# First weights side by side in one array, first products by kind, and sums of squares through transposes, in a one-core encoder layer

## The chip, the core and the metric

The kernel runs on one core of one Trainium2 chip. A core has five engines, each with an instruction queue of its own: TensorE (PE in the profile; PEld is its loading of weights) multiplies matrices into PSUM, VectorE (DVE) and ScalarE (ACT) do element-wise work, GpSimd (POOL) does element-wise work more slowly, SyncE (SP) only issues transfers. Transfers between the chip's memory (HBM) and the core's memory (SBUF) are made by 16 DMA engines; SP and ACT put them on their queues. The metric is the device time of one execution in microseconds (us), as a median of several runs; lower is better.

## The reference

One layer of an encoder on 1024 tokens of width 1024, in float32:

```python
hn   = rmsnorm(h, norm_mix)
proj = hn @ w_in                       # 18 tiles of 128 columns
o_a  = window_gqa_sink(...)            # |i-j| <= 128, a sink logit for each head
o_b  = neighbourhood_attention(...)    # 8 x 16 window on a 16 x 64 grid
mix  = concat(rmsnorm(o_a, norm_a), rmsnorm(o_b, norm_b))
h    = h + mix @ w_out
hn   = rmsnorm(h, norm_ffn)
h    = h + (silu(conv3(hn @ w_gate)) * (hn @ w_up)) @ w_down
out  = rmsnorm(h, norm_final)
```

`rmsnorm(x, g)` is `x / sqrt(mean(x*x) + 1e-6) * g` over the 1024 (or 512) features of a token. `proj` is split into the parts of both attention groups; group A rotates part of each head. All other details are the same in both kernels and play no part here.

## The kernel before

**Layout and products.** Features lie on the 128 partitions and tokens along the rows: `xT` is eight tiles `xts[k]` of 128 x 1024. A float32 product is made as three products of a rounded type: each operand is split into a high part (ACT rounds it) and a low part (DVE subtracts), and `block` (lines 167 to 170) adds high weight by high x, high weight by low x, and low weight by high x into one PSUM bank, each for 512 tokens. `tsl(h)` is half h of the tokens. So one weight tile needs, for each k and half, three matrix products with 512 columns.

**The start.** The first three tiles of `w_in` (projections 0, 1 and 2, the list `first`) are not run one after another but side by side, k by k, as x arrives, into six PSUM banks (two each with the tags `pj`, `o`, `s`). Lines 84 to 122 write the transfers: `w_in` is laid out as [tile, partition, k, column], so each of the three tiles has its own transfers, for k=0, k=1, k=2..3 and k=4..7 (`steps`), between the transfers of x. All are issued by SP, but the second half of `xts[0]` and `par` (120 columns of small parameters: norm gains, convolution weights) by ACT. `pin` keeps the marked instructions in the written order on their queues. Lines 580 to 621 write the splits: `split_x` scales x by the gain from `par` and splits it, `split_first_w` splits the weights of one tile and step (ACT the high part, DVE the low part), and `add_square` squares each x tile on ACT and adds up the squares on DVE in `acc`. Nine warm-up products (`WARM`, line 137) run on PE before the first operands are there.

The products are written in lines 636 to 649: for k=0 to 5 both halves and three tiles, then the last two k (`TAIL`) tile by tile. After the first tile's first half come two calls of `inverse_narrow` on `acc`; after the second tile's first half come two of `widen`.

**The norms.** `inverse_narrow` (lines 194 to 204) turns a tile of squares (features on partitions, tokens along the row) into `1/sqrt(mean + eps)` with tokens on partitions: for each block of 128 tokens a matrix product with the squares as the stationary operand and one column of `ones` (each 1/1024), a square root on ACT and a reciprocal on DVE. `widen` spreads that back over all partitions with a transpose for each block. The calls are: a pair for the first norm, a pair for group A (`narrow_a`, `wide_a`), a pair for group B (lines 841 to 847), a single one for each half of the second norm (lines 953 and 1099), one for a half of the last norm (line 1368), and two with n=2 and two tiles of squares each for the quarters of the other half (lines 1385 and 1390).

**The end.** The last product of `w_down` for the second four output tiles is made in two quarters of 256 tokens. `leave_quarter` adds a quarter of PSUM to the residual and squares it into `parts`; for the tile before the last it also adds the sum of the squares of all earlier tiles. `finish` widens the norm twice (DVE reads one bank, ACT copies the other for GpSimd), scales and issues the output.

**What sets the order.** PE's instructions run exactly in the order in which they are written (line 127). Instructions of ACT, DVE, POOL and SP that aren't pinned are put in order ahead of time by a planner, from estimated times and priorities; `tc.high_priority(offset)` moves an instruction ahead in it, `tc.issue_after` behind a named one. In the attention stage, projections fill in between attention units by rates written out by hand (`RATES`). The SBUF pools have a fixed number of buffers for each tag: 8 `mix` and 14 `op` tiles of 128 x 1024, 2 `raw`, 3 `whi`, 3 `wlo`.

## Time and profile before

| | |
|---|---|
| median of 3 runs | 1087.69 us (1087.55 to 1088.12) |
| the profiled execution | 1088.62 us, its span 1086.8 us |
| instructions | 14983, of them 5144 matrix products |
| mean granted clock of PE | 0.997 |
| busy share of the span | PE 98%, weight load 82%, DVE 79%, ACT 51%, POOL 10% |
| DMA | 144.94 MB moved, mean 133 GB/s |

The span runs from the first to the last instruction of the profiled execution; all row times below count from its start. A row of the timeline reads: start in us, duration in us, engine, line of the kernel, operation, what it writes `<-` what it reads, shape, and how many neighbouring instructions of that kind the row merges; in brackets the idle time of the engine in front of it and what ended it. SPq and ACTq are the issuing of transfers. Durations of matrix products overlap, since they are pipelined; the distance from start to start is what one costs. The lines themselves stand in the prediction.

### The profile page before, as it was taken

To read this page: it belongs to the slowest core of one execution; us is meant where nothing else is said; L and a number is where in the kernel's file an instruction comes from. 1 tells how busy PE (TensorE), PEld (TensorE's weight loads), DVE (VectorE), ACT (ScalarE), POOL (GpSimd) and SP (SyncE) were. 2 spreads that over 40 slices of the span, in tenths; PEclk is the share of its full clock that TensorE was granted. 3 is DMA by queue.
4 is the path that set the end of the run, shared out by engine and by line. 5 is a ranking of instruction groups with operands and counts; after the bars stand their busy time and mean duration, and the time that the engine had idled before them with its cause. 6 is when DMAs were issued, how large, how long until landed. Compare 5 with 4: busy or idle time off the path is not lost.

```text
span 1086.8 us, 14983 instructions
## 1 busy us (share of the span) xinstructions
PE 1070.2 (98%) x5144; PEld 895.0 (82%) x5144; DVE 860.1 (79%) x1570; ACT 554.5 (51%) x1047; POOL 105.0 (10%) x188
## 2 busy tenths in 40 slices
PE   8999999999999999999999999999999999999997
PEld 7888888888888888887788888888888888888887
DVE  6789787667788688899998877877887867897764
ACT  7457676556676545545434334342433645444451
POOL 0223332222232100000000000000000000000001
PEclk9999999999999999999999999999999999999998
DMA  8223022232225147214342222323322788867644
GB/s 275 73 73 88 30 68 59 78 77 78 78 68 161 65 137 249 88 39 157 134 146 107 107 107 97 120 95 111 111 88 97 244 297 295 272 214 241 227 129 155
DMA packets 69084, 144.94 MB, mean 133 GB/s; under 512 B 8208, under 2 KB 19600, under 8 KB 69008
## 3 DMA queue, kind: packets, MB, share of 16 engines
q1 hardware_dynamic: 58784, 118.43, 34.6%
q10 hardware_dynamic: 10224, 25.56, 6.2%
q8 instruction: 40, 0.66, 0.3%
q14 instruction: 36, 0.29, 0.1%
HBM read 103.58 MB, written 28.57 MB: 122 GB/s over the span
## 4 chain that ended last, share of the span: by engine, by line
PE 88%; DVE 8%; ACT 2%; DMA 1%; issue 1%; SPq 0%; POOL 0%; DVEq 0%; ACTq 0%; POOLq 0%
PE pj L168 7%; PE pj L169 7%; PE pj L170 7%; PE dn L883 6%; PE dn L885 6%; PE dn L884 6%; PE z L885 5%; PE z L884 5%; PE z L883 5%; PE s L344 3%; PE x L883 3%; PE x L884 3%; PE x L885 3%; PE y L885 3%; PE y L884 3%; PE y L883 3%
## 5 line engine op out<-in xcount | busy, mean ns | idle before, releaser
L872 ACT ACTIVATE whi<-ws 128x512 fp32r<-128x512 f32 (+1 forms) x100 | 60.3, 623 | 127.8 <-DVE ws L990 80.5
L883 PE MATMUL dn<-xd,whi 128*128 128x512 f32 (+1 forms) x330 | 124.1, 376 | 0.0
L885 PE MATMUL dn<-xd,wlo 128*128 128x512 f32 (+1 forms) x330 | 123.7, 375 | 0.0
L884 PE MATMUL dn<-xd,whi 128*128 128x512 f32 (+1 forms) x330 | 123.7, 375 | 0.0
L168 PE MATMUL pj<-xgh,whi 128*128 128x512 f32 x248 | 104.4, 421 | 1.0 <-ACT xgh L584 1.0
L885 PE MATMUL z<-hg,wlo 128*128 128x512 f32 x264 | 103.0, 390 | 0.7 <-DVE wlo L873 0.7
L883 PE MATMUL z<-hg,whi 128*128 128x512 f32 x264 | 102.9, 390 | 0.0
L884 PE MATMUL z<-hg,whi 128*128 128x512 f32 x264 | 102.7, 389 | 0.0
L370 ACT ACTIVATE p<-p,nm 128x385 f32<-128x385 f32 (+3 forms) x128 | 75.1, 587 | 50.4 <-DVE nm L366 49.3
L169 PE MATMUL pj<-xgl,whi 128*128 128x512 f32 x248 | 97.5, 393 | 0.9 <-DVE xgl L585 0.8
L170 PE MATMUL pj<-xgh,wlo 128*128 128x512 f32 x248 | 97.6, 394 | 0.0
L374 POOL TENSOR_SCALAR p<-p,sm 128x384 f32<-128x384 f32 (+1 forms) x128 | 74.9, 598 | 219.3 <-DVE sm L372 204.7
L873 DVE TENSOR_TENSOR wlo<-raw,whi 128x512 fp32r<-128x512 f32 (+1 forms) x102 | 66.4, 671 | 26.6 <-ACT whi L872 26.4
L872 ACT ACTIVATE whi<-raw 128x512 fp32r<-128x512 f32 (+1 forms) x102 | 60.6, 612 | 45.2 <-DMA raw<-in_w_down_dram 20.0
L873 DVE TENSOR_TENSOR wlo<-ws,whi 128x512 fp32r<-128x512 f32 (+1 forms) x100 | 66.9, 681 | 21.0 <-ACT whi L872 20.8
L380 DVE TENSOR_TENSOR pl<-pt,ph 128x384 fp32r<-128x384 f32 (+2 forms) x108 | 63.3, 589 | 24.3 <-ACT ph L379 23.0
L1307 POOL TENSOR_TENSOR h<-h,wide 128x256 f32<-128x256 f32 (+1 forms) x6 | 5.4, 924 | 709.9 <-ACT wide L1303 709.9
L379 ACT ACTIVATE ph<-pt 128x384 fp32r<-128x384 f32 (+2 forms) x108 | 55.2, 514 | 32.2 <-PE pt L479 25.1
L885 PEld LDWEIGHTS dn<-xd,wlo 128*128 128x128 f32 x330 | 62.1, 188 | 11.3
L884 PEld LDWEIGHTS dn<-xd,whi 128*128 128x128 f32 x330 | 62.1, 188 | 11.1
L883 PEld LDWEIGHTS dn<-xd,whi 128*128 128x128 f32 x330 | 62.1, 188 | 11.1
L1198 ACT ACTIVATE xd<-xd 128x512 fp32r<-128x512 f32 x77 | 47.5, 626 | 44.0 <-DMA xd<-x 43.2
(220 smaller groups left out, 2671.2 us busy)
## 6 DMA issues: line engine op xcount, KB each, us to landing
xd<-x SPq DMA_DIRECT2D x77, 256.0 KB, 4.6
raw<-in_w_down_dram SPq DMA_DIRECT2D x72, 256.0 KB, 3.6
raw<-in_w_gate_dram SPq DMA_DIRECT2D x22, 512.0 KB, 3.4
raw<-in_w_up_dram SPq DMA_DIRECT2D x22, 512.0 KB, 3.8
x<-c ACTq DMA_DIRECT2D x22, 512.0 KB, 3.5
raw<-in_w_in_dram SPq DMA_DIRECT2D x30, 256.0 KB, 2.9
raw<-in_w_down_dram SPq DMA_DIRECT2D x36, 192.0 KB, 3.8
x<-t ACTq DMA_DIRECT2D x11, 512.0 KB, 2.6
```

Source lines behind the costliest of these rows:

```text
L168: nc.tensor.matmul(ps, w[0], x[0][:, tsl(h)], start=first, stop=False)
L169: nc.tensor.matmul(ps, w[0], x[1][:, tsl(h)], start=False, stop=False)
L170: nc.tensor.matmul(ps, w[1], x[0][:, tsl(h)], start=False, stop=last)
L370: nc.scalar.activation(p[:, j, 0:e], p[:, j, 0:e], AF.Exp, bias=nm, scale=-1.0, accum_out=sm[:, j:j + 1])
L374: nc.gpsimd.tensor_scalar(p[:, i, 0:m], p[:, i, 0:m], sm[:, i:i + 1], 1.0, op0=ALU.mult, op1=ALU.mult)
L379: nc.scalar.activation(ph[:, 0:n], ps[:, 0:n], AF.Copy)
L380: nc.vector.tensor_tensor(pl[:, 0:n], ps[:, 0:n], f32(ph[:, 0:n]), op=ALU.subtract)
L872: nc.scalar.activation(hi, src, AF.Copy)
L873: nc.vector.tensor_tensor(lo, src, f32(hi[:, :, :]), op=ALU.subtract)
L883: nc.tensor.matmul(ps, w[0], x[0], start=first and i == 0, stop=False, skip_group_check=True)
L884: nc.tensor.matmul(ps, w[0], x[1], start=False, stop=False, skip_group_check=True)
L885: nc.tensor.matmul(ps, w[1], x[0], start=False, stop=last and i == len(ws) - 1, skip_group_check=True)
```

## The change

The change has six parts.

1. The weights of the first three tiles leave `w_in` for an array of their own, `w_first`, laid out as [partition, k, 384]: for each k the 128 columns of all three tiles lie side by side. Five transfers (k=0, 1, 2..3, 4..5, 6..7) replace twelve. The raw tiles and the splits move to other buffers (two `raw`, three `op`, five `mix`). `w_in` starts at tile 3.
2. Of `par`, the eight columns of the first norm's gain are loaded first, by ACT's queue; the other 112 after them, also there. The second half of `xts[0]` goes to SP's queue. The order of loads is x0 first half, w0, x0 second half, w1, x1 in halves, w2..3, x2, x3, w4..5, x4, x5, w6..7, x6, x7.
3. The first weights are split for each k in one piece of 384 columns, k=0 with the high part on DVE, just ahead of that k's x.
4. The first half of k=0 is multiplied by kind: high by high for three tiles, then low weight by high x, then high weight by low x. Warm-up products fall from nine to seven.
5. `inverse_narrow` with a single tile of squares transposes the blocks on PE, sums them on DVE along the row, and takes root and reciprocal as before, all with high priority; with two tiles it stays as it was. The copy of the first norm (`rstd1`) also gets high priority.
6. At the end, `finish` widens once unless it is the last quarter's. For the first quarter `leave_quarter` adds the last tile's squares to those of the tile before, so that the quarter's norm has a single tile of squares; it is made after the second of three groups in place of the first, and `finish` after the third in place of the second.

```diff
-WARM = 9
+WARM = 7
...
-        steps = [slice(0, 1), slice(1, 2), slice(2, 4), slice(4, 8)]
-        load_x(0, tsl(0))
-        nc.scalar.dma_start(par[:, 0:C_SINK], small)
-        load_x(0, tsl(1), nc.scalar)
-        for m in range(3):
-            load_first_w(m, steps[0])
...
+        FIRST = [slice(0, 1), slice(1, 2), slice(2, 4), slice(4, 6), slice(6, 8)]
...
+        def load_first_w(i):
+            ks = FIRST[i]
+            pin(nc.sync.dma_start(raws[i], w_first[:, ks, :]))
+
+        pin(nc.scalar.dma_start(par[:, 0:KT], small[:, 0:KT]))
         load_x(0, tsl(0))
+        load_first_w(0)
+        load_x(0, tsl(1))
+        load_first_w(1)
         load_x(1, tsl(0))
         load_x(1, tsl(1))
+        load_first_w(2)
+        for i, k in ((3, 2), (4, 4)):
             load_x(k)
+            load_x(k + 1)
+            load_first_w(i)
+        load_x(6)
+        load_x(7)
+        pin(nc.scalar.dma_start(par[:, KT:C_SINK], small[:, KT:C_SINK]))
...
         def inverse_narrow(sqs, dim, tag, n=4):
             ps = bank("ss", tag)
+            v = cpool.tile([128, n], F32, name="v4", tag="v4", bufs=4, padded_shape=[128, 4])
+            if len(sqs) == 1:
+                for c in range(n):
+                    nc.tensor.transpose(ps[:, c * 128:(c + 1) * 128], sqs[0][:, c * 128:(c + 1) * 128], ident)
+                with tc.high_priority(offset=500):
+                    nc.vector.tensor_reduce(v, ps[:, 0:n * 128].rearrange("p (c w) -> p c w", w=128), axis=mybir.AxisListType.X, op=ALU.add)
+                    nc.scalar.activation(v, v, AF.Sqrt, bias=eps, scale=1.0 / dim)
+            else:
+                for i, sq in enumerate(sqs):
+                    for c in range(n):
+                        nc.tensor.matmul(ps[:, c:c + 1], sq[:, c * 128:(c + 1) * 128], ones[:, 0:1], start=c == 0 and i == 0,
+                                         stop=i == len(sqs) - 1, skip_group_check=True)
+                with tc.high_priority(offset=500):
+                    nc.scalar.activation(v[:, 0:n], ps[:, 0:n], AF.Sqrt, bias=eps, scale=float(D) / dim)
+            with tc.high_priority(offset=500):
+                nc.vector.reciprocal(v[:, 0:n], v[:, 0:n])
             return v
...
+        def hi_first_w(k, queue):
+            i, raw = next((i, r) for i, r in enumerate(FIRST) if r.start <= k < r.stop)
+            raw = raws[i][:, k - raw.start]
+            if queue is nc.vector:
+                pin(queue.tensor_copy(his[k], raw))
+            else:
+                pin(queue.activation(his[k], raw, AF.Copy))
+            return raw
+
+        def split_first_w(k, queue=nc.scalar):
+            raw = hi_first_w(k, queue)
+            pin(nc.vector.tensor_tensor(los[k], raw, f32(his[k]), op=ALU.subtract))
...
+        split_first_w(0, nc.vector)
         split_x(0, tsl(0))
         split_x(0, tsl(1))
+        split_first_w(1)
         for h in range(2):
             split_x(1, tsl(h))
         acc = add_square(xts[0], None)
         for k in range(2, KT):
+            split_first_w(k)
             split_x(k)
             acc = add_square(xts[k - 1], acc)
...
+        for part in range(3):
+            for p, ps in zip(first, banks):
+                w, x = p.w[0], xg[0]
+                nc.tensor.matmul(ps[0], w[part == 1], x[part == 2][:, tsl(0)], start=part == 0, stop=False)
         for k in range(KT - TAIL):
-            for h in range(2):
+            for h in range(k == 0, 2):
...
-            wide, again = widen(v, "pt", n), widen(v, "pt", n)
+            wide = widen(v, "pt", n)
+            again = widen(v, "pt", n) if split else wide
...
             if j + NP < KT - 1:
                 nc.vector.tensor_tensor(s2, s2, sq[0][:, cols], op=ALU.add)
+            elif cols.start == 0:
+                nc.vector.tensor_tensor(s2, s2, parts[0, j - 1], op=ALU.add)
...
-                    if (k, j, c) == (1, 2, 0):
-                        vs[0] = inverse_narrow([parts[0, 2], parts[0, 3]], D, "s", 2)
                     if (k, j, c) == (1, 2, 1):
+                        vs[0] = inverse_narrow([parts[0, 3]], D, "s", 2)
+                    if (k, j, c) == (1, 2, 2):
                         finish(0, vs[0], quarters[0])
...
+        "w_first": w_in[0:3].transpose(1, 2, 0, 3).reshape(128, KT, 384),
+        "w_in": w_in[3:],
```

More of the change, by code (lines that the diff above doesn't have):

```diff
@@ L89, in load_x @@
             pin(queue.dma_start(xts[k][:, part], xT[k, :, part]))
-        def halves(name, dt=F32):
-            t = big(name, "mix", dt)[:, :].rearrange("p (k c) -> p k c", c=128)
-            return t[:, 0:4], t[:, 4:8]
-        raws = [wpool.tile([128, 4, 128], F32, name="raw", tag="raw", bufs=2) for _ in range(2)]
-        his, los = ([wpool.tile([128, 4, 128], F32R, name=n, tag=n) for _ in range(3)] for n in ("whi", "wlo"))
-        (r3, r3b), r12, h12, l12, (h3, l3) = halves("r3"), halves("r12"), halves("h12", F32R), halves("l12", F32R), halves("w3", F32R)
@@ L111, in hybrid_layer @@
-        for m in range(3):
-            load_first_w(m, steps[1])
+        FIRST = [slice(0, 1), slice(1, 2), slice(2, 4), slice(4, 6), slice(6, 8)]
+        flat = lambda t, n: t[:, 0:n * 384].rearrange("p (k c) -> p k c", c=384)
+        raws = [wpool.tile([128, HALF], F32, name="raw", tag="raw", bufs=2) for _ in range(2)]
+        raws = [flat(t[:, :], 1) for t in raws] + [flat(big("r", "op")[:, :], 2) for _ in range(3)]
+        his, los = ([wpool.tile([128, HALF], F32R, name=n, tag=n)[:, 0:384] for _ in range(3)] for n in ("whi", "wlo"))
```

50 lines of the change are left out of this document (15 added, 35 removed).

## The prediction

> **What bounds the kernel now.** I read the page's engine shares and chain, then who TensorE (PE) waited for, then the start row by row, since the change lies there and at nine short reductions.
>
> ```profile
> PE 1070.2 (98%) x5144; PEld 895.0 (82%) x5144; DVE 860.1 (79%) x1570; ACT 554.5 (51%) x1047; POOL 105.0 (10%) x188
> PE 88%; DVE 8%; ACT 2%; DMA 1%; issue 1%; SPq 0%; POOL 0%; DVEq 0%; ACTq 0%; POOLq 0%
> ```
>
> PE is busy for 98% of the 1086.8 us span and makes 88% of the chain that ended last. Its order is written by hand, so a PE instruction that goes away moves all behind it forward, as long as nothing else comes late. The waits of PE:
>
> ```profile
> PE o L491 <- DVE pl L380: 1.4, 4, 0.6
> ...
> PE pj L168 <- ACT xgh L584: 1.0, 1, 1.0
> PE pj L169 <- DVE xgl L585: 0.8, 1, 0.8
> ```
>
> The columns are total us, times and the longest. The first is the largest of the attention stage, the last two are the start, which in order of time reads:
>
> ```profile
> 0.74 0.39 SPq L89 DMA_DIRECT2D xt<-in_xT_dram  x1
> ...
> 4.00 0.72 ACT L584 ACTIVATE xgh<-xt,par 128x512 fp32r<-128x512 f32 x1 [0.84 <-DMA par<-in_small_dram]
> ...
> 4.97 0.50 PE L168 MATMUL pj<-xgh,whi 128*128 128x512 f32 x1
> ...
> 6.14 0.39 PE L168 MATMUL o<-xgh,whi 128*128 128x512 f32 x1
> ...
> 6.74 0.90 SPq L89 DMA_DIRECT2D xt<-in_xT_dram  x2
> ...
> 13.44 0.39 PE L170 MATMUL s<-xgh,wlo 128*128 128x512 f32 x1
> 13.58 1.15 ACT L584 ACTIVATE xgh<-xt,par 128x1024 fp32r<-128x1024 f32 x1 [1.61 <-DMA xt<-in_xT_dram]
> ...
> 14.76 1.28 DVE L585 SCALAR_TENSOR_TENSOR xgl<-xt,par,xgh 128x1024 fp32r<-128x1024 f32 x1 [3.29 <-ACT xgh L584]
> ...
> 16.10 0.50 PE L169 MATMUL pj<-xgl,whi 128*128 128x512 f32 x1 [0.82 <-DVE xgl L585]
> ...
> 32.45 1.21 DVE L597 TENSOR_TENSOR sq<-sq 128x1024 f32<-128x1024 f32 x1
> ...
> 33.71 1.95 PE L199 MATMUL ss<-ones,sq 128*128 128x1 f32 x16
> ...
> 35.52 0.47 PE L168 MATMUL pj<-xgh,h 128*128 128x512 f32 x1
> ...
> 35.99 0.18 DVE L203 RECIPROCAL v<-v 128x4 f32<-128x4 f32 x1 [0.72 <-ACT v L202]
> ```
>
> The third tile of x (k=2) lands at 13.58, and PE stands until its high and low parts are made. From the first product at 4.97 to the first reduction at 33.71 PE needs 28.74 us for 114 products (six k of 18, and six of the last two k). From 6.14 to 13.44 there are 32 steps without a gap, 0.228 us each; at that pace 26.0 would do, and 2.7 are lost. VectorE (DVE) meanwhile makes the low parts and the running sum of squares, which that reduction reads; its last addition ends at 33.66.
>
> ```profile
> 3.00:11.00 8.00, 7.91 (x36) 6.53 (x35) 4.80 (x12) 5.33 (x15) 0.00 (x0) 1.00 0.95 269
> 11.00:14.00 3.00, 2.82 (x13) 2.01 (x11) 0.43 (x1) 1.39 (x3) 0.00 (x0) 1.00 0.99 360
> 14.70:33.70 19.00, 18.11 (x78) 14.56 (x78) 18.94 (x19) 15.88 (x19) 3.59 (x2) 1.00 0.57 210
> ```
>
> In these windows the columns are length, busy us of PE, weight load, DVE, ACT and POOL, granted clock, DMA share and GB/s. Before 14.7 the transfers are the limit (DMA share 0.95 and 0.99); after it DVE is, busy for 18.94 of 19.00. So the start has two limits, and gaining on PE alone stops at DVE.
>
> **Part 1, the loads.** Twelve weight loads become five, x's second half goes from ACT's queue to SP's, and SP issues 15 transfers instead of 21. Two small loads, 8 columns and then 112, take the place of one on ACT's queue. Ahead of k=2 SP had 12 issues from 0.74 to 6.74, 0.5 each; now it has seven, so k=2 is issued at about 4.2, 2.5 earlier. If issuing decided alone, k=2 would land near 11.0. By bytes, x0, x1, x2 and the weights of four k come first, with the small parameters: 2.42 MB, before and after. The sum of the GB/s rows reaches that at about 11 us, and k=2 was seen 2.5 later. Without the hole that the issues leave, the 360 GB/s of the second window bounds the rate from above and 269 from below. With 0.25 MB moved by 3.0, the bytes are there between 9.0 and 11.0; with 1.5 to 2.5 for the landing this gives 10.5 to 13.5. I take 11.5, between the issue bound and the bytes, a gain of 2.1.
>
> **Part 2, the splits.** DVE's chain to the first reduction moves with k=2, but its weights grow: per k one low part of 128x384 where three tiles' halves stood.
>
> ```profile
> 10.21 0.75 DVE L590 TENSOR_TENSOR wlo<-raw,whi 128x256 fp32r<-128x256 f32 x2
> ...
> 18.29 1.29 DVE L590 TENSOR_TENSOR l<-r,h 128x512 fp32r<-128x512 f32 x2
> ```
>
> Two overlap a little, which gives 0.35 or so a piece for 256 columns and 0.6 for 512, so 0.48 for 384, an estimate. From k=2 on, five of them (k=3 to 7) are 2.4 where three 512s took 1.8: +0.6. The last addition ends at 33.66 - 2.1 + 0.6 = 32.16. PE's own path is shorter. The first operands come with less in front of them: `par` falls from 120 columns (60 KB) to 8 (4 KB), and the 0.84 of ACT's wait for it goes or shrinks, but ACT now needs x and DVE the first weights, so I let the first product start at 4.7 (4.4 to 5.2). Running all `hi` by `hi` products first, then `lo` weights, then `lo` x gives DVE 1.4 us before its slowest result is due, so the stalls at 5.2 to 6.1 go. PE reaches the reduction at 4.7 + 26.0 + 0.3 = 31.0 and waits for DVE until 32.16. Gain at that point 33.71 - 32.16 = **1.55**. Bounds: 2.7 if DVE isn't the limit, -0.45 if k=2 lands at 13.5 again. Two fewer warm-up products (WARM) cost nothing while operands are later than their end.
>
> **Part 3, the sums.** A single reduction of four column blocks was four products with a one-column operand, two records each. It becomes four transposes, a DVE sum and the same root and reciprocal.
>
> ```profile
> 277.56 1.84 PE L199 MATMUL ss<-ones,sq 128*128 128x1 f32 x16
> 279.27 0.48 PE L168 MATMUL pj<-xgh,whi 128*128 128x512 f32 x1
> ...
> 423.09 0.95 PE L199 MATMUL ss<-ones,s 128*128 128x1 f32 x8
> 423.90 0.49 PE L168 MATMUL pj<-mgh,wo 128*128 128x512 f32 x1
> ...
> 38.37 1.03 PE L210 MATMUL sw<-cst,v 128*128 128x128 f32 x8
> 39.16 0.47 PE L168 MATMUL o<-xgh,h 128*128 128x512 f32 x1
> ...
> 426.76 0.60 PE L210 MATMUL sw<-cst,v 128*128 128x128 f32 x4
> 427.12 0.48 PE L168 MATMUL pj<-mgh,wo 128*128 128x512 f32 x1
> ```
>
> From start to start, a pair of reductions takes 1.81 at 33.71 and 1.71 at 277.56, a single one 0.81; eight transposes take 0.79, four 0.36. There are three pairs (first norm, group A, group B): (1.81 - 0.79) + 2 x (1.71 - 0.79) = 2.86. Three singles (both halves of the second norm, one of the last): 3 x 0.45 = 1.35. Together **4.2** of PE. The Trainium skill, "TensorE: Matmul & The Clock Gate", Part 4, speaks against this edit: it gives about 275 ns for a transpose in a kernel. By that the 36 transposes would cost 9.9, more than the products that they replace, and the 4.2 would be a loss of about 2. This trace disagrees: 0.79 / 8 is 0.10 each, so I give that outcome no chance.
>
> Each single reduction adds one DVE sum out of PSUM, 128x512; the nearest rows are a subtraction and an addition from SBUF (L590 some 0.65 for 512, L597 1.21 for 1024), so 0.7. Its cover is the PE work between reduction and widening: 12 products, 2.7 us, at the first norm; the same 12 at group B, 2.9 us at 423.90 to 426.76, more elsewhere. At the first norm a pair's second reciprocal now ends 36.17 - 33.71 = 2.46 after the pair began; less 1.02 of products and with 0.7 for the sum that is 2.1 after the start and 1.35 after the transposes, 2.05 if the second sum has to follow the first. Either fits; each 0.1 that it is late costs 0.1. Behind the sums on DVE's queue stand evacuations and splits, which PE waits for at a few places only (above). Nothing to 3.5 in all, rival (d); I take 0.
>
> **Part 4, the end.** The first quarter's reduction of two sums becomes one of two transposes, after one more DVE addition, and is made one group later.
>
> ```profile
> 1059.55 1.03 PE L210 MATMUL sw<-cst,v 128*128 128x128 f32 x8
> 1060.35 0.36 PE L883 MATMUL dn<-xd,whi 128*128 128x256 f32 x1
> ...
> 1069.77 0.95 PE L199 MATMUL ss<-ones,s 128*128 128x1 f32 x8
> 1070.59 0.36 PE L883 MATMUL dn<-xd,whi 128*128 128x256 f32 x1
> ...
> 1072.52 2.44 DVE L1309 SCALAR_TENSOR_TENSOR h<-h,par,sw 128x256 f32<-128x256 f32 x6 [1.29 <-PE sw L210]
> ...
> 1080.42 2.44 DVE L1309 SCALAR_TENSOR_TENSOR h<-h,par,sw 128x256 f32<-128x256 f32 x6 [0.63 <-PE sw L210]
> ```
>
> The reduction falls from 0.82 to 0.18 (two transposes): 0.64. The second widening is dropped: 0.80 to 0.36 for the half, 0.36 to 0.18 for the quarter: 0.62. Against it, only nine 256-column products (1.1, half the pace's 0.228 each) now lie between reduction and widening, and the chain of 1.35, with a sum of half the width (-0.3), takes 1.05 to 1.25: -0.1. What hangs on that widening (DVE's scaling, GpSimd, eight output transfers on SP's queue) moves one group, 1.1, later; the last quarter's own scaling starts 7.9 after the first's, so they keep clear. The last quarter keeps its form. Sum **1.15**.
>
> **Sum.** 1.55 + 4.2 + 1.15 = 6.9. The profiled execution took 1088.62 (span 1086.8), 0.93 over the median of the runs, so 1081.7 as it was taken and **1080.8** as a median: 1087.69 - 6.9.
>
> **Rivals.** (a) *Transfers keep their pace*, k=2 lands near 13.5. For: DMA share 0.95 already. Against: the issues spread over six us. Term of the start -0.45: 1082.8.
> (b) *DVE isn't the limit of the start*, because fewer, longer instructions or a better place for other weights' splits save it a microsecond. Term 2.7: 1079.6.
> (c) *PE starts cold.* The warm-up's weight loads are slow:
>
> ```profile
> L138 PEld LDWEIGHTS warm_ps<-ones x18: 288/333/338, 1.0 to 4.6; 128*128 128x128 f32 x18
> L199 PEld LDWEIGHTS ss<-ones,sq x48: 186/192/192, 33.7 to 382.5; 128*128 128x128 f32 x48
> ```
>
> 333 ns against 192 for the same form later, and only the last is quicker, so the array speeds up at about 4.8, after 3.8 us of work, though the granted clock reads 1.00. Fourteen records instead of 18 end at 4.1. If the pause to 4.7 starts the count again, 3.8 us run at half pace: 1.9 lost, of which the 1.15 that PE waits for DVE anyway absorbs most: 1081.6. The Trainium skill, same page, Part 1, has this rule (half rate until one busy window of some 3.4 us); by its figure the loss would be 1.7 before absorption.
> (d) *The sums come late*: DVE serves them behind other work and PE waits 0.5 at each of seven widenings, 3.5: 1084.3. For: DVE 79% busy. Against: high priority, covers of 2.7.
> (e) *Slower: the attention stage loses its fit.* ACT, DVE and POOL instructions that aren't pinned are put in order by a planner from estimated times; new ones change that. PE's place to lose is the wait of the second value product (L491) for `pl`:
>
> ```profile
> L380 DVE TENSOR_TENSOR pl<-pt,ph 128x384 fp32r<-128x384 f32 (+2 forms) x108 | 63.3, 589 | 24.3 <-ACT ph L379 23.0
> ```
>
> It is made 108 times, and four waits for it average 0.35. It decides from 20 further waits of that size (7.0). At a third of the 108 it costs 12.6: 1093.4. Against: PE's order and the stage's balance stay, and the edit touches one pair of sums in it.
>
> **Numbers.** Forecast 0.50, (a) 0.14, (b) 0.12, (c) 0.06, (d) 0.10, (e) 0.08. The range 1078.8 to 1085.0 holds the first five with the bounds of the start and of the sums; (e) and a bad (d) lie outside. A measurement here tells 0.2% (2.2 us) from no change: faster 0.86, the same 0.06 (the part of (d) and a mild (e) above 1085.5), slower 0.08.
>
> **What would show it.** Right: k=2's first ACT row near 11.5; PE reaching the first reduction near 32, with a wait for the sum of squares; pairs of transposes of 0.79; no PE wait of over 0.3 at a widening but the last two. Wrong: k=2 near 13.5; new waits at L491 or at a widening; first products 0.43 apart.

## The result and the profile after

| | before | after |
|---|---|---|
| median | 1087.72 us (1086.77 to 1088.12, 6 runs) | 1082.76 us (1082.01 to 1083.54, 6 runs) |
| the profiled execution | 1088.62, span 1086.8 | 1082.01, span 1080.2 |
| ratio of the runs | | 0.9955, 95% interval 0.9944 to 0.9967 |

The kernel became 4.96 us faster, where 6.9 were forecast. The two profiled executions lie 6.6 apart: before's is 0.90 above its median, after's 0.75 below its own. By the two profiles' pages PE still makes most of the chain. Of the changed kernel:

```profile
PE 1064.6 (99%) x5092; PEld 889.0 (82%) x5092; DVE 866.3 (80%) x1578; ACT 553.8 (51%) x1042; POOL 103.6 (10%) x188
PE 85%; DVE 9%; ACT 3%; DMA 1%; issue 1%; POOL 0%; DVEq 0%; SPq 0%; ACTq 0%; POOLq 0%
```

PE lost 5.6 us of busy time (1070.2 to 1064.6) and 52 products; DVE and ACT have a larger share of the chain. Whom PE waited for (us in total, times, longest):

```profile
PE o L501 <- DVE pl L390: 1.5, 4, 0.6
PE vt L307 <- DVE pl L390: 1.4, 2, 1.1
...
PE sw L220 <- DVE v L213: 1.1, 3, 0.6
```

The waits for k=2 of x (1.0 and 0.8 before) are gone, the two of the attention stage stand as they were (1.5 and 1.4, before 1.4 and 1.4), and the widenings `sw` now wait three times, 1.1 in all, where they waited once, 0.6. The start in order of time:

```profile
5.22 0.63 PE L653 MATMUL o<-xgh,whi 128*128 128x512 f32 x1
...
5.65 0.63 PE L653 MATMUL s<-xgh,whi 128*128 128x512 f32 x1
...
6.36 0.39 PE L653 MATMUL o<-xgh,wlo 128*128 128x512 f32 x1
...
10.31 1.15 ACT L594 ACTIVATE xgh<-xt,par 128x1024 fp32r<-128x1024 f32 x1
11.50 1.28 DVE L595 SCALAR_TENSOR_TENSOR xgl<-xt,par,xgh 128x1024 fp32r<-128x1024 f32 x1 [0.73 <-ACT xgh L594]
...
29.71 1.21 DVE L617 TENSOR_TENSOR sq<-sq 128x1024 f32<-128x1024 f32 x1
...
31.32 1.03 PE L201 MATMUL ss<-cst,sq 128*128 128x128 f32 x8
...
32.11 0.48 PE L169 MATMUL pj<-xgh,h 128*128 128x512 f32 x1
...
32.69 0.63 ACT L161 ACTIVATE whi<-raw 128x512 fp32r<-128x512 f32 x1 [5.95 <-DMA raw<-in_w_in_dram]
33.34 1.28 ACT L204 ACT_TABLE_LOAD   x1
34.63 0.49 ACT L204 ACTIVATE v<-v,eps 128x4 f32<-128x4 f32 x2
34.96 0.18 DVE L213 RECIPROCAL v<-v 128x4 f32<-128x4 f32 x1 [1.72 <-ACT v L204]
35.28 1.29 PE L220 MATMUL sw<-cst,v 128*128 128x128 f32 x8 [0.18 <-DVE v L213]
```

k=2 is split at 10.31 without a wait for its transfer (13.58 before), the last addition of squares ends at 29.71 + 1.21 = 30.92 (33.66 before), and the reduction comes at 31.32 (33.71). The first products run 0.43 apart at first, and from 6.36 on at 0.23. Ahead of the widening at 35.28 the square root stands on ACT's queue behind a split of weights that waited 5.95 for its transfer, and behind the load of the root's table. The same windows as in the prediction (length, busy PE, weight load, DVE, ACT, POOL, granted clock, DMA share, GB/s):

```profile
3.00:11.00 8.00, 7.69 (x32) 6.28 (x31) 4.87 (x8) 5.55 (x9) 0.00 (x0) 1.00 1.03 347
11.00:14.00 3.00, 3.00 (x15) 2.49 (x14) 2.50 (x3) 3.00 (x5) 0.00 (x0) 1.00 1.03 421
```

The transfers rose from 269 to 347 GB/s up to 11 us, and from 360 to 421 after it.

Where the 6.6 of the two profiles came from can be read from PE alone, since its order is written by hand: the start of the same row in both, and the difference from the place before.

| place | before | after | gain so far | added | forecast |
|---|---|---|---|---|---|
| first reduction | 33.71 | 31.32 | 2.39 | 2.39 | 1.55 |
| first transposes of v, behind the first norm | 43.35 | 40.54 | 2.81 | 0.42 | 1.02 |
| group A, sums | 277.56 | 274.78 | 2.78 | -0.03 | 0 |
| group A, widening | 285.90 | 282.23 | 3.67 | 0.89 | 0.92 |
| group B, widening | 385.44 | 381.27 | 4.17 | 0.50 | 0.92 |
| second norm, first half's widening | 426.76 | 422.15 | 4.61 | 0.44 | 0.45 |
| second norm, second half's widening | 452.66 | 447.59 | 5.07 | 0.46 | 0.45 |
| a product `z` of the up weights | 505.06 | 500.43 | 4.63 | -0.44 | 0 |
| last norm, half's widening | 1059.55 | 1054.43 | 5.12 | 0.49 | 0.45 |
| last reduction | 1078.69 | 1072.45 | 6.24 | 1.12 | 1.15 |
| end of the span | 1086.8 | 1080.2 | 6.6 | 0.4 | 0 |

The start gave more than forecast, two of the three pairs of sums gave about half, the third pair, the single sums and the end gave what was forecast, and 0.44 were lost again at 500 us, where DVE waited for a transfer:

```profile
498.95 0.69 DVE L941 TENSOR_TENSOR ws<-raw 128x512 f32<-128x512 f32 x1 [0.54 <-DMA raw<-in_w_up_dram]
...
500.43 0.50 PE L902 MATMUL z<-hg,whi 128*128 128x512 f32 x1 [0.24 <-ACT whi L891]
```

The time from the last widening to the last output landing (6.86 before, 6.5 here) lies between 6.5 and 7.0 in all fourteen profiles, and a second profile of the changed kernel has 6.99, so the last 0.4 is scatter and not the edit's.

### The profile page after: what moved, and what is told of

It reads as the page before. It is cut to its first block, busy times and chain, and to the rows that moved or that the text cites. A ratio compares the mean times of both kernels' runs of the same rounds, so it can differ in the third digit from the quotient of the medians.

```text
span 1080.2 us, 14876 instructions
## 1 busy us (share of the span) xinstructions
PE 1064.6 (99%) x5092; PEld 889.0 (82%) x5092; DVE 866.3 (80%) x1578; ACT 553.8 (51%) x1042; POOL 103.6 (10%) x188
## 4 chain that ended last, share of the span: by engine, by line
PE 85%; DVE 9%; ACT 3%; DMA 1%; issue 1%; POOL 0%; DVEq 0%; SPq 0%; ACTq 0%; POOLq 0%
PE pj L169 7%; PE pj L171 7%; PE pj L170 7%; PE dn L904 7%; PE dn L903 6%; PE dn L902 6%; PE z L904 5%; PE z L902 5%; PE z L903 5%; PE s L354 3%; PE x L902 3%; PE x L903 3%; PE x L904 3%; PE y L904 3%; PE y L902 3%; PE y L903 3%
```

## The experiments

"Before" is the time of the kernel before, measured along with the run on the same chip. The intervals reach 0.9 to 1.6 us to either side, so two runs whose times differ by less than about 1 us are told apart by their rows alone.

| run | us, median (range, runs) | before | ratio, 95% interval |
|---|---|---|---|
| start_only | 1086.13 (1085.73 to 1089.25, 11) | 1088.3 | 0.9986 [0.9977, 0.9995] |
| sums_only | 1085.69 (1084.44 to 1087.39, 8) | 1088.3 | 0.9975 [0.9965, 0.9986] |
| end_only | 1086.9 (1086.4 to 1088.12, 11) | 1088.3 | 0.9989 [0.998, 0.9997] |
| after_again | 1082.37 (1081.98 to 1083.15, 5) | 1088.3 | 0.9947 [0.9934, 0.9959] |
| sqrt2 | 1081.39 (1080.81 to 1083.6, 4) | 1087.7 | 0.9942 [0.9928, 0.9957] |
| warm9 | 1082.54 (1081.95 to 1083.63, 4) | 1087.7 | 0.995 [0.9936, 0.9965] |
| three | 1086.2 (1083.98 to 1092.35, 10) | 1087.7 | 0.9986 [0.9972, 1.0001] |
| byblock | 1082.82 (1081.6 to 1083.69, 4) | 1087.7 | 0.9951 [0.9936, 0.9966] |
| sqrt3 | 1082.35 (1080.91 to 1084.01, 5) | 1088.11 | 0.9948 [0.9935, 0.996] |
| after_third | 1082.77 (1082.08 to 1083.59, 5) | 1088.11 | 0.9951 [0.9938, 0.9965] |
| sqrt3_warm9 | 1081.78 (1080.68 to 1081.8, 5) | 1088.49 | 0.9937 [0.9923, 0.995] |
| sqrt3_again | 1081.33 (1080.33 to 1083.44, 5) | 1088.49 | 0.9937 [0.9924, 0.9949] |

### One part alone

start_only has the loads, the splits and the first products of the change, on the kernel before:

```diff
+        FIRST = [slice(0, 1), slice(1, 2), slice(2, 4), slice(4, 6), slice(6, 8)]
...
+        split_first_w(0, nc.vector)
...
+        for part in range(3):
+            for p, ps in zip(first, banks):
```

> Only the start is changed (loads, splits, products by kind, two fewer warm-up products); the reductions and the end are as before. Theory A (the parts add up, each PE microsecond goes through): the first reduction starts near 31.3 instead of 33.71, the same distance stays up to the end, and the time falls by 2.0 to 2.8 us. Theory B (what the start gains is taken back where a transfer is due, since those keep their own pace): the same 31.3, but the distance shrinks at a later wait for a transfer and less than 1.5 us is left.

sums_only has the reduction through transposes and its priorities alone:

```diff
+            if len(sqs) == 1:
+                for c in range(n):
+                    nc.tensor.transpose(ps[:, c * 128:(c + 1) * 128], sqs[0][:, c * 128:(c + 1) * 128], ident)
```

> Only the reductions with one tile of squares go through transposes, and the copy of the first norm has its priority. Theory A: PE reaches the last reduction 3.4 to 4.2 us earlier (4.2 less what it waits at the widenings), time down by as much; at the first norm no wait at the widening, since the root's table is loaded early there, as before. Theory B (late sums): waits of 0.5 or more at several widenings, less than 2.5 us left.

end_only has the later first quarter and its single widening:

```diff
-            wide, again = widen(v, "pt", n), widen(v, "pt", n)
+            wide = widen(v, "pt", n)
+            again = widen(v, "pt", n) if split else wide
...
+                    if (k, j, c) == (1, 2, 2):
                         finish(0, vs[0], quarters[0])
```

> Only the end is changed: one widening fewer, and the first quarter's norm from one tile of squares, with the old one-column products (four records in place of eight). Theory A: 0.41 for the products and 0.62 for the widenings, less 0.1 to 0.3 for the wait at the widening: 0.7 to 0.9 us faster. Rival: the outputs of the first quarter, issued one group later, push the last ones back, and nothing is left.

after_again is the changed kernel, measured along with the three parts.

> The changed kernel once more, to see in a second profile which of its distances to the kernel before are the same each time. Theory A: 5 us less as a median; up to the group A norm the starts of PE agree with the first profile of it to 0.1 us. Theory B (transfers take back a part that differs from run to run): the rows agree in the attention stage, and differ by 0.4 or more after the waits for weights near 500 us or at the start or the last landing.

The medians are 2.17, 2.61 and 1.40 below before's 1088.3, together 6.18; the whole change is 5.93 below it. Within these intervals the parts add up; whether one takes back some tenths of another the medians can't show. after_again's own rows agree with neither theory alone: its first reduction comes 0.44 earlier than in the first profile (30.88), from the transposes of v to group A it is 0.19 earlier, and the last landing takes 0.49 longer.

start_only is as theory A has it in its first reduction (31.00) and its median, but not all of the distance stays. Its rows are 2.71 ahead of before's at the first reduction and 2.70 at the widening of the second norm's second half (449.96), and 2.15 at the widening of the last norm (1057.40). Ahead of that widening PE waits for DVE:

```profile
1048.90 1.05 PE L200 MATMUL ss<-ones,s 128*128 128x1 f32 x8 [0.21 <-DVE s L1298]
```

The profile of the whole change has no such wait there. end_only gave more than the 0.7 to 0.9 of its theory A: from the last norm's widening (1058.99) to the last reduction (1077.03) it is 18.04, before 19.14, so 1.10 by the rows.

The forecast had 1.55, 4.2 and 1.15, so by the medians it is the sums that are short, by 1.6; sums_only's 2.61 lies between its two theories. By its rows 0.97 is missing at the first norm and 0.43 at group B (4.03 from reduction to widening, before 4.52). The first norm's pair shows why:

```profile
33.00 1.09 PE L200 MATMUL ss<-cst,sq 128*128 128x128 f32 x8
...
37.35 1.29 PE L219 MATMUL sw<-cst,v 128*128 128x128 f32 x8 [0.49 <-DVE v L212]
...
42.59 1.03 PE L306 MATMUL vt<-cst,t 128*128 128x128 f32 x8
```

```profile
34.75 0.63 ACT L160 ACTIVATE whi<-raw 128x512 fp32r<-128x512 f32 x1 [5.52 <-DMA raw<-in_w_in_dram]
35.40 1.28 ACT L203 ACT_TABLE_LOAD   x1
```

In the profile of the kernel before, the load of the root's table stood ahead of the sums:

```profile
29.95 1.28 ACT L202 ACT_TABLE_LOAD   x1
```

The expectation that it would stay early was wrong: with the new sums it comes behind them and behind a split that waits for its transfer. From the reduction to the transposes of v it is 9.59, in the kernel before 43.35 - 33.71 = 9.64: of the 1.02 that the cheaper reduction frees, 0.05 are left. In the rows are a wait of 0.49 ahead of the widening, and 1.29 instead of 1.03 for its eight transposes, since the second reciprocal is late too; the other 0.2 stand between the two rows.

### An early load of the root's table

sqrt2 adds two idle roots to the changed kernel, each only to have the table loaded:

```diff
         acc = add_square(xts[KT - 1], acc)
+        pin(nc.scalar.activation(warm, eps, AF.Sqrt))
...
                 nc.vector.tensor_tensor(last[:, tsl(h)], last[:, tsl(h)], sums["b"][:, tsl(h)], op=ALU.add)
+            nc.scalar.activation(warm, eps, AF.Sqrt)
```

> The changed kernel with two idle square roots of the constant `eps` on ACT, one pinned behind the last square of the start, one with high priority behind the last squares of group B, so that the table of the root is loaded (1.28 us) before the sums are there. Theory A (ACT is late: the root stands on its queue behind a weights' split that waited 5.95 us for its transfer, and then behind the table load): the root at the first norm follows DVE's sums directly, the waits of 0.18 and some 0.26 inside the widening at 35.28 and of 0.24 at group B's widening (381.27) go, and the kernel is 0.4 to 0.8 us faster than the changed one: about 1081.9 where the changed kernel has 1082.5. Theory B (the sums themselves are late on DVE, behind other work): the widenings come at the same distance from their sums, 3.96 and 4.03 us, and the time is the same.

At the first norm the rows are as theory A has them. The table comes at 26.88, in the time in which ACT waited anyway, the root follows the weights' split at once, and the widening has no wait:

```profile
26.88 1.28 ACT L636 ACT_TABLE_LOAD   x1
28.17 0.20 ACT L636 ACTIVATE warm<-eps 128x1 f32<-128x1 f32 x1
...
31.64 1.09 PE L201 MATMUL ss<-cst,sq 128*128 128x128 f32 x8 [0.41 <-DVE sq L617]
...
33.32 0.63 ACT L161 ACTIVATE whi<-raw 128x512 fp32r<-128x512 f32 x1 [4.43 <-DMA raw<-in_w_in_dram]
33.86 0.47 ACT L204 ACTIVATE v<-v,eps 128x4 f32<-128x4 f32 x2
...
35.34 1.03 PE L220 MATMUL sw<-cst,v 128*128 128x128 f32 x8
...
40.33 1.03 PE L307 MATMUL vt<-cst,t 128*128 128x128 f32 x8
```

The widening comes 3.70 after its sums, with transposes of 1.03, instead of 3.96 and 1.29. From the reduction (31.64) to the transposes of v (40.33) it is 8.69 now, 0.95 less than the 9.64 before, where 1.02 were forecast.

How late the norm is depends on more than the table: on how long after the reduction the split's transfer lands. The profile of the changed kernel in which that is the same is after_third's:

```profile
30.97 1.09 PE L201 MATMUL ss<-cst,sq 128*128 128x128 f32 x8
...
32.66 0.63 ACT L161 ACTIVATE whi<-raw 128x512 fp32r<-128x512 f32 x1 [5.94 <-DMA raw<-in_w_in_dram]
...
40.49 1.03 PE L307 MATMUL vt<-cst,t 128*128 128x128 f32 x8
```

There the split starts 1.69 after the reduction, in sqrt2 1.68, and the distance to the transposes of v is 9.52 there and 8.69 here. So the moved load is worth 0.83 at this place. Counted from the start of the span little of it shows (40.33 against 40.49), because in sqrt2's profile the data of the start came some 0.6 later.

At group B nothing changed (4.03 and a wait of 0.24): the second idle root depends on nothing but a constant, and the planner put it at 45.0 us. The time, 1081.39, is 1.15 below that of warm9, measured along with it, but the intervals of the two overlap, and the loss at 500 us, some 0.4, is absent from this profile and from byblock's too and so doesn't belong to the edit. The time alone therefore doesn't settle what the edit is worth.

sqrt3 makes the second root read what it is to stand behind:

```diff
-            nc.scalar.activation(warm, eps, AF.Sqrt)
+            nc.scalar.activation(warm, last[:, 0:1], AF.Sqrt)
```

> The first idle root of the run before stays; the second, which the planner had put at 45 us, now reads one column of group B's squares and so stands behind them, ahead of the weights' splits on ACT. In the written order the first reciprocal then follows DVE's two sums directly, where two evacuations and splits stood between. Theory A (the root's table and the order that it brings made group B's widening late): the wait of 0.24 there goes and the widening comes 3.7 to 3.8 us after its sums instead of 4.03; with the first norm's wait gone too the kernel takes 0.6 to 1.3 us less than the changed one in the same call, about 1081.4. Theory B (only the start counted): 3.8 to 4.1 us at group B, and 0.3 to 0.8 less than the changed one.

The changed kernel had, at group B (its rows first, sqrt3_again's behind them; sqrt3's own profile has the same distances):

```profile
377.24 1.03 PE L201 MATMUL ss<-cst,sq 128*128 128x128 f32 x8
...
378.35 1.28 ACT L204 ACT_TABLE_LOAD   x1
379.65 0.52 ACT L204 ACTIVATE v<-v,eps 128x4 f32<-128x4 f32 x2
380.35 0.68 DVE L857 TENSOR_TENSOR wo<-raw,wo 128x512 fp32r<-128x512 f32 x1
...
380.95 0.23 DVE L213 RECIPROCAL v<-v 128x4 f32<-128x4 f32 x2
381.27 0.62 PE L220 MATMUL sw<-cst,v 128*128 128x128 f32 x4 [0.24 <-DVE v L213]
```

```profile
376.88 1.03 PE L201 MATMUL ss<-cst,sq 128*128 128x128 f32 x8
...
380.50 0.60 PE L220 MATMUL sw<-cst,v 128*128 128x128 f32 x4
```

By the rows theory A held here as well: 3.62 instead of 4.03 (it had 3.7 to 3.8), and no wait. Before it was 4.52, so this pair now gains 0.90 where 0.92 were forecast. Two causes lie in the rows of the changed kernel: the table load keeps the first root from following its sum, and DVE's reciprocals, 0.23 in all, stand behind an evacuation and a split (380.35). The roots are over at 380.17 and DVE turns to the reciprocals at 380.95, so there it is DVE's order that came last, and not the table load. Both went with this edit, since the planner set the sums and the reciprocals earlier too (the latter from 378.79 on in sqrt3_again); it doesn't part them. The time doesn't decide between the theories: 1082.35 is only 0.42 below the changed kernel's 1082.77 beside it, which is in B's range. Its profiled run is its slowest, 1084.01, and shows something else, which follows below.

> The changed kernel itself, for its time beside the run above and a third profile: 1082.4 to 1082.8; first reduction 30.8 to 32.1, the gap to the first widening 3.7 to 4.2, the array's turn to full pace anywhere between 4.8 and 7 us.

after_third gave 1082.77, a first reduction at 30.97, a widening 4.29 after it and the turn to full pace by 4.63, the last two just outside what was expected. It also has a wait that the first profile lacks: 0.28 at the widening of the second norm's first half (422.34). warm9, byblock and sqrt3 wait there too, 0.29 to 0.47.

### The loads in fifteen pieces

three leaves the order and the bytes as the change has them, and cuts each load of the first weights in three:

```diff
-            pin(nc.sync.dma_start(raws[i], w_first[:, ks, :]))
+            for m in range(3):
+                cs = slice(128 * m, 128 * m + 128)
+                pin(nc.sync.dma_start(raws[i][:, :, cs], w_first[:, ks, cs]))
```

> The changed kernel with each of the five loads of the first weights split into three transfers of 128 columns each (15 instead of 5 on SP's queue, rows of 512 bytes instead of 1536), with the same bytes in the same order. Theory A (the number of issues and the length of the rows held the transfers back): ten more issues of 0.5 us, six of them ahead of k=2, put k=2's first ACT row back from 10.3 to 12.5 or 13.5; the first reduction comes at 33 to 34 instead of 31.3, and 2.0 to 2.7 us are lost: about 1084.8. Theory B (the order and the small first load of parameters brought the gain): k=2 stays within 0.6 of 10.3 and the time within 0.5 us.

Its windows, and its k=2:

```profile
7.00:11.00 4.00, 4.00 (x20) 3.30 (x19) 2.68 (x4) 2.97 (x5) 0.00 (x0) 1.00 0.89 292
11.00:14.00 3.00, 3.00 (x15) 2.37 (x13) 0.56 (x1) 1.58 (x3) 0.00 (x0) 1.00 0.89 273
```

```profile
7.24 0.94 SPq L89 DMA_DIRECT2D xt<-in_xT_dram  x2
...
12.89 1.15 ACT L596 ACTIVATE xgh<-xt,par 128x1024 fp32r<-128x1024 f32 x1 [1.42 <-DMA xt<-in_xT_dram]
...
33.58 1.09 PE L203 MATMUL ss<-cst,sq 128*128 128x128 f32 x8 [0.40 <-DVE sq L619]
```

Theory A: with 128 columns a row instead of 384, and ten issues more, k=2 is issued at 7.24 (4.04 in the changed kernel) and split at 12.89, the transfers run at 273 GB/s where the changed kernel had 421, and the first reduction is back at 33.58. The 12.89 is in the range of the three profiles with the old loads, 12.87 to 13.58. So the order and the small first load alone don't bring the gain of the start; it needs the fewer, longer transfers. Which of the two, the issues or the length of a row, this run doesn't part; with its 25 issues on SP's queue it has more than the 21 of the kernel before, so some gain of the order may be hidden in it. It also lost 1.4 behind the start, at the second norm, where PE waited 0.52 and 0.90 for DVE; this wasn't expected, and makes its total 1086.2 where 1084.8 was.

### Nine warm-up products, and the first products by tile

```diff
-WARM = 7
+WARM = 9
```

> The changed kernel with nine warm-up products again. Profiles so far, with the start of the first product at full pace: with nine, 5.0, 5.4 and 6.9 us; with seven, 4.9, 4.9 and 6.3. Theory A (the moment at which the array speeds up is set by something that doesn't follow the number of warm-up products): the first product comes when its operands are there or when the warm-up ends, whichever is later (4.9 to 5.1), the pace turns to 0.23 anywhere between 4.9 and 7, and the time is that of the changed kernel within 0.4 us. Theory B (seven leave the array cold, nine don't): the first products run 0.23 apart from the first on, and the kernel is 0.3 to 0.7 us faster than the changed one.

Theory A: the first product came at 4.86, the array was slow until 6.99 (the first weight load of 0.19), so nine can leave it slow as seven can, and the time (1082.54) is that of the changed kernel in the other measurements (1082.37 to 1082.77). More profiles of this kind follow below.

byblock writes the first half of k=0 tile by tile:

```diff
-        for part in range(3):
-            for p, ps in zip(first, banks):
-                w, x = p.w[0], xg[0]
-                nc.tensor.matmul(ps[0], w[part == 1], x[part == 2][:, tsl(0)], start=part == 0, stop=False)
         for k in range(KT - TAIL):
-            for h in range(k == 0, 2):
+            for h in range(2):
```

> The changed kernel with the first half of k=0 multiplied tile by tile again (high by high, high by low x, low by high x) and not by kind. Theory A (PE is the limit of the changed start, so each stall there counts): the second product waits for the low part of x, which DVE ends at about 5.8 to 6.0 us, so 0.6 to 0.8 us are lost ahead of the second product, the first reduction moves from 31.3 (30.9 in the second profile) to about 31.7, and the kernel is 0.4 to 0.8 us slower than the changed one. Theory B (DVE is still the limit, its last addition 30.92 against PE's 31.32): the loss is soaked up by a wait for the sum of squares, and the time stays within 0.2 us.

```profile
6.33 0.50 PE L170 MATMUL pj<-xgl,whi 128*128 128x512 f32 x1 [0.69 <-DVE xgl L595]
...
32.08 1.04 PE L201 MATMUL ss<-cst,sq 128*128 128x128 f32 x8
32.87 0.63 ACT L161 ACTIVATE whi<-raw 128x512 fp32r<-128x512 f32 x1 [6.01 <-DMA raw<-in_w_in_dram]
33.52 1.28 ACT L204 ACT_TABLE_LOAD   x1
...
35.70 1.05 PE L220 MATMUL sw<-cst,v 128*128 128x128 f32 x8
```

Neither theory as it was put. The stall of 0.69 is there, and the reduction moves to 32.08, 0.8 to 1.2 later than in the three profiles of the changed kernel, as A has it. But the widening comes only 0.4 to 0.6 later, without a wait, and the time, 1082.82, is within 0.3 of warm9's beside it. What soaks it up isn't DVE's sum of squares, as B has it, but ACT: the split of weights that waits for its transfer until 32.87, and the table load behind it, don't come earlier when PE does, and the widening comes behind them. With the table load left on the path, a quicker start of PE is worth half of what it looks, or less. Eleven profiles in the order of that delay show it:

| profile | table load behind the split | split starts after the reduction by | reduction to the transposes of v |
|---|---|---|---|
| three | yes | 1.83 | 9.69 |
| sums_only | yes | 1.75 | 9.59 |
| after_third | yes | 1.69 | 9.52 |
| after_again | yes | 1.62 | 9.47 |
| after | yes | 1.37 | 9.22 |
| warm9 | yes | 1.16 | 8.98 |
| byblock | yes | 0.79 | 8.62 |
| sqrt2 | no | 1.68 | 8.69 |
| sqrt3_warm9 | no | 1.52 | 8.59 |
| sqrt3_again | no | 1.31 | 8.61 |
| sqrt3 | no | -0.10 | 8.61 |

With the load behind the split the distance grows with the delay; with the load moved it stays at 8.6 to 8.7.

### The moment at which the array speeds up

sqrt3's profile has the shortest distance to its widenings, and the latest first reduction of the profiles with the change's start and loads, 33.26. Its first products:

```profile
4.87 0.76 PE L654 MATMUL pj<-xgh,whi 128*128 128x512 f32 x1 [0.52 <-DVE whi L601]
...
9.70 0.56 PE L171 MATMUL pj<-xgh,wlo 128*128 128x512 f32 x1
10.09 0.39 PE L169 MATMUL o<-xgh,whi 128*128 128x512 f32 x1
```

They run 0.43 apart until 9.7, while the granted clock reads 1.00 in every window. Twelve profiles, in which "turn" is the start of the first weight load of 0.19 us (others before it take 0.3); byblock and three, which the table leaves out, turn by 5.13 and 5.83:

| profile | start code, warm-up products | turn | k=2 split from | DVE's last addition ends | first reduction |
|---|---|---|---|---|---|
| before | old, 9 | 4.97 | 13.58 | 33.66 | 33.71 |
| sums_only | old, 9 | 5.55 | 12.87 | 32.94 | 33.00 |
| end_only | old, 9 | 6.88 | 13.35 | 33.44 | 33.49 |
| after_third | new, 7 | 4.63 | 10.29 | 30.91 | 30.97 |
| sqrt2 | new, 7 | 4.78 | 10.95 | 31.59 | 31.64 |
| start_only | new, 7 | 4.92 | 10.32 | 30.94 | 31.00 |
| after_again | new, 7 | 4.98 | 10.10 | 30.73 | 30.88 |
| after | new, 7 | 6.36 | 10.31 | 30.92 | 31.32 |
| sqrt3_warm9 | new, 9 | 6.61 | 10.69 | 31.33 | 31.57 |
| sqrt3_again | new, 7 | 6.91 | 10.58 | 31.20 | 31.67 |
| warm9 | new, 9 | 6.99 | 10.79 | 31.44 | 32.03 |
| sqrt3 | new, 7 | 10.10 | 10.76 | 31.39 | 33.26 |

With the old start the turn doesn't matter: PE waits for k=2 anyway, and the reduction follows DVE's last addition by 0.05. With the new one it follows DVE by 0.05 to 0.15 where the turn comes by 5, and PE is the limit where it comes later: 0.24 to 0.59 behind DVE at 6.4 to 7.0, 1.87 at 10.1. The better start has brought PE and DVE to within half a microsecond, and so made the kernel sensitive to a moment that differs from run to run.

The Trainium skill, "TensorE: Matmul & The Clock Gate", Part 1, says that the array runs at half rate until one busy window of some 3.4 us has passed, and that the windows run free of the kernel's start. With nine products PE is busy without a gap from 0.99, so by that the turn falls, as an estimate, between 0.99 + 3.4 = 4.4 and 0.99 + 6.8 = 7.8; the five profiles with nine, 4.97 to 6.99, agree. The scatter of 500 ns to either side that the page gives is too small for this: here the five lie 2 us apart.

With seven there is a gap of 0.3 to 0.6 ahead of the first product (0.81 in byblock, 1.67 in three), and one turn of the nine profiles with seven, 10.10, lies outside those bounds. Whether the gap did that was the question of the last two runs: sqrt3 again, and sqrt3 with `WARM = 9`.

> The same kernel with seven warm-up products: 1081.0 to 1082.5 as a median; the widening of the first norm at most 3.8 us after its sums, of group B 3.6 to 3.7 as in the first profile; the turn to full pace between 4.6 and 10 us.

> The kernel with both idle roots, and nine warm-up products. In one profile with seven, PE stood idle from 4.35 to 4.87 and the array came to full pace only at 9.95; in the profiles with nine, where no such gap is, at 4.8, 5.4, 6.8 and 6.9. Theory A (the gap can break the count, so that seven risk a far later turn): with nine the turn is never later than 7.9, the widest run lies at most 2 us above the narrowest, and the median is 0.3 to 1.0 us below that of the same kernel with seven beside it. Theory B (the moment falls anywhere with either number, or the odd late turn is too rare to count): the medians agree within 0.4 us and the spreads are alike.

Open. The medians, 1081.33 with seven and 1081.78 with nine, lie the other way round than A has it, and 0.45 apart, just more than B's 0.4. The five runs with nine lie within 1.1, the ten with seven (sqrt3 and sqrt3_again) within 3.7, 1080.33 to 1084.01, which is A's side; but the turn was seen in three profiles only (6.61 with nine, 10.10 and 6.91 with seven), and a broken count was seen once.

sqrt3_warm9 is the version I would keep, 0.9937 of the kernel before; that nine is better than seven in it isn't shown. All five of its runs (at most 1081.8) are faster than the fastest of the sixteen of the changed kernel (1081.98), though those were measured at other times, and the intervals of the ratios overlap, 0.9923 to 0.995 against 0.9944 to 0.9967.

## Why the prediction was right, and where it was off

The forecast was 1080.8 with a range of 1078.8 to 1085.0; the time is 1082.76. The mechanisms of the three parts hold, and three sizes were off. Two of them nearly cancel: the start paid 0.84 more than forecast and the late sums 1.0 less. Neither was foreseen, so that the total came as near as it did is in part luck.

**The loads.** "I take 11.5" for k=2: it was 10.31, and 10.10 to 10.95 in all ten profiles of the new loads, in six of them without a wait for the transfer. The step that failed is "the 360 GB/s of the second window bounds the rate from above". That rate was itself held down by the row length or the issues, which three shows by bringing it back to 273 to 292. With the new loads it was 421 in that window. The Trainium skill, "DMA: Bandwidth & Descriptors", section "Where 436 GB/s comes from", gives 435 as the ceiling of the ports, and says that for loads from HBM some 358 bind; the window from 11 to 14 us has 421, so here, with one core at work, the measurement is against 358 as a bound and below the first.

**The splits.** From the low part of k=2 to the last addition DVE took 30.92 - 11.50 = 19.42, before 33.66 - 14.76 = 18.90: +0.52, forecast +0.6. So DVE ends 3.26 earlier by the transfers and 0.52 later by its weights. The reading that PE waits for DVE at the first reduction was right where the array is quick by 5 us (the reduction 0.05 to 0.15 behind DVE), and wrong in the profile shown, where rival (c)'s slow products make PE the limit at 31.32. The term was 1.55, and 2.39 came, near rival (b)'s 2.7, but for another reason: DVE saved nothing, its data came earlier.

**Cold start.** Rival (c) was half right. The slow products are there, in five of the nine profiles with the new start, and cost 0.2 to 1.9. But taking away two warm-up products isn't needed for them: both profiles with nine and the new start have them, and so have two of the three with the old start, where they cost nothing. Whether it had a part in the one turn at 10.10 stays open.

**The sums.** The terms for PE were right: eight transposes take 0.79 (the next product starts at 32.11, the first transpose at 31.32), and the undisturbed places gained 0.89, 0.44, 0.46 and 0.49 where 0.92 and 0.45 were forecast. What failed is "Either fits", and the "I take 0" behind it, for the first norm and group B: they gained 0.42 and 0.50, 1.0 less in all. The working put the end of the first norm's second reciprocal 2.1 after the start of the sums; it was 35.80 - 31.32 = 4.48. It counted DVE's sum, the root and the reciprocal, but not what stands ahead of them on their queues. In the kernel before, the table load stood at 29.95, before the sums, and so no row of the path had its 1.28; the new order put it after a weights' split that waits for a transfer. At group B it was, last of all, an evacuation and a split on DVE's queue. That is rival (d) at two of its seven places, 0.60 and 0.42 against its 0.5 each, and in after_third's profile at a third, 0.28. With the load moved, the waits at the two places are gone. At the first norm sqrt2 shows the load's share, 0.83 at the same delay of the split's transfer; at group B the load's share and that of DVE's order aren't parted.

**The end.** 1.12 against 1.15; alone, without the transposes, it had 1.10 by the rows and 1.40 as a median.

**The attention stage.** Rival (e) fell: the waits for `pl` are 1.5 and 1.4 where they were 1.4 and 1.4.

**What is left.** By the profiles the late sums cost 1.0 and the loss at 500 us 0.44; the start paid 0.84 more than forecast. The changed kernel's three medians are 4.96, 5.93 and 5.34 below before's beside them, 1.0 to 1.9 short of the forecast. The kernels with both idle roots are 6.71 (nine warm-up products) and 7.16 (seven) below it, and sqrt3, the latter's first measurement, 5.76. That this is about the forecast is again the start's surplus as much as the mended sums. Why the unprofiled runs of the changed kernel spread over 1.6 us wasn't seen in their traces; the turn of the array is one cause that the profiles show.

## What to carry to other kernels

A short helper chain between engines is not priced by its instructions: look in the trace for what stands ahead of each of them on its queue, table loads among it, and ask whether the edit moves that. And compare such a chain only between profiles in which the transfers that it waits for lie alike. A rate seen in a window bounds nothing from above as long as the transfers there are short and their issue late. When two limits lie within half a microsecond, a further gain on one of them is half hidden by the other, and what was harmless before (here the moment at which the array speeds up) begins to show.

## What the runs showed of the hardware

- The array came to full pace between 4.6 and 10.1 us of the span, with the same start code; until then a weight load takes about 0.3 instead of 0.19 and products are 0.43 apart instead of 0.23, while the granted clock reads 1.00.
- Loads in rows of 1536 bytes and more moved 421 GB/s over 3 us, with a DMA share of 1.03; with the weights in rows of 512 bytes, and ten issues more, it was 273 at a share of 0.89.
- A table load on ACT took 1.28 in each place, and an idle activation of one column, 0.20, was enough to move it in this kernel; where it read only a constant the planner put it at 45.0 us, and where it read group B's squares it stood behind them.
